# Attention scores of two softmax maps computed as couples, with 64-row matmuls for the small terms

## The chip, the cores and the metric

The kernel runs on one core of a Trainium2 chip. Its engines work side by side and are held together by semaphores: TensorE (PE) multiplies matrices into PSUM, VectorE (DVE), ScalarE (ACT) and GpSimd (POOL) work on rows, SyncE (SP) issues most of the DMAs. The metric is the device time of one execution in microseconds (us).

## What is computed

One encoder layer is applied to two sequences, of 2048 and of 1024 tokens, with the same weights. Its parts are an input projection, a convolution branch, an attention branch, a gated merge, an output projection and a layer norm. The change concerns the attention branch, which has 4 heads; each has two maps of scores over 64 features, and values of 128 features:

```python
def block(q_blk):
    s = jnp.einsum('bqhcd,bkhcd->bhcqk', q_blk, k).astype(jnp.float32) * scale
    p = jax.nn.softmax(s, axis=-1)
    a = p[:, :, 0] - lam * p[:, :, 1]
    return jnp.einsum('bhqk,bkhe->bqhe', a.astype(v.dtype), v)
```

## The kernel before

The kernel has three stages. The first projects the inputs and leaves queries, keys, values and gates in device memory. The second is the attention, from about 1437 to 2150 us of the profiled execution. The third merges and projects. Only the second is touched, and the loads that it makes.

**Numbers in two halves.** TensorE multiplies in a format with fewer bits than float32. So each operand is split into a high half (rounded to that format) and a low half (what is left). Queries and keys are stored as such halves in `qd` and `kd`, by half, then 128 rows (64 of map 0, 64 of map 1), then tokens.

**Scores.** `Head.keys` loads for a map `c` and 1024 keys a tile `km`: the high half on the upper 64 partitions, the low half on the lower 64. `Pair.load` loads for each map two tiles `qq` of 256 queries: the high half twice, one copy above the other, and the low half twice. `score(p, j, c, hf)` (lines 798 to 812) takes 128 queries (`j` = 0 or 1 of a pair), one map `c` and 1024 keys (`hf`). It makes four matmuls into the PSUM tile `s` (1024 columns, two buffers): for each 512 columns one with the high queries and one with the low ones, each over all 128 rows. So all four products of halves are summed, low times low among them. VectorE then scales `s`, takes the running maximum and writes it into the tile `e` (line 810), an eviction.

**Softmax and difference.** `soften` (line 821) takes the exponential on ScalarE with the sum of the row. `combine` (lines 824 to 830) takes the reciprocal of the sum of map 1 on VectorE (line 827); GpSimd multiplies it with the sum of map 0 (828), scales the tile of map 1 (829) and adds it to the tile of map 0 (830). From then on only the tile of map 0 is needed.

**Product with the values.** `turn` (line 832) transposes 256 keys of both query tiles of a pair on TensorE into `tp` (PSUM, two buffers), and ScalarE copies the high half into `ah` (839). `rest` (844) makes the low half `al` on VectorE. `product` makes six matmuls with the values into `ops` through `mm3` (lines 99 to 101). `squares` and `sums` take the sums of squares that the later norm needs.

**Buffers of scores.** `e` has `NE` = 8 buffers of 2048 columns. In the long group (2048 keys, 32 pairs of query tiles, 8 steps each) each map of each query tile has a buffer of its own. That of map 1 comes free when line 830 has read it; that of map 0, when the last turn of its pair has. A tile that is written into a used buffer waits on its engine until the former use is over. In the short group (16 pairs, 4 steps each) both maps lie in one buffer. `live[0]` counts the buffers that are taken, in the order in which the work is written.

**The order.** The `while` loop writes the order of TensorE, VectorE, ScalarE and GpSimd by hand (`manual_schedule`); each engine works strictly in it. A pass, or step, `now`, issues in this order: a score if one is left and `live` allows it; the turn of an earlier pair with its `ah`; what waits in `mid` for this step (exponentials); the product of the turn two steps earlier; the `al` of this step's turn; and what waits in `late` (a `combine`, `sums`). `p.at` says when a pair's turns may begin: `LAGS` steps after its last score. The exponential comes one step after its last score, `combine` at the end of the step after that. Every fourth step a piece of the next stage's weights is loaded and split (`resident`), for the first 128 steps.

Of the kernel before, what the change touches and what calls it, by code (L numbers as in the profile page):

```python
# [11 lines left out]
F32 = mybir.dt.float32  # L12
F32R = mybir.dt.float32r
AF = mybir.ActivationFunctionType
ALU = mybir.AluOpType
# [3 lines left out]
P = 128  # L19
# [7 lines left out]
HD = 64  # L27
# [4 lines left out]
EPS = 1e-5  # L32
SCALE = 1.0 / math.sqrt(HD)
KAPPA = 2.0 ** -11
LAGS = (8, 8)
NE = 8
NST = NH * sum(LENS) // P
ROOT_MAX = 1.8446742e19
# [5 lines left out]
def encoder_kernel(ctx: ExitStack, tc: tile.TileContext, t: dict):  # L44
    nc = tc.nc
# [25 lines left out]
    qd, kd, vd, sd, sr, ud, cgd, agd, mcd, mad, ogd, ssqd, rrd = ([] for _ in range(13))  # L71
# [34 lines left out]
    kvp, vp = [], []  # L106

    class Head:
# [4 lines left out]
        def keys(self, c):  # L113
            for hf in range(LENS[self.g] // 1024):
                self.km[c, hf] = kk = kvp[0].tile([P, 1024], F32R, name="km", bufs=6)
                for i in range(2):
                    nc.sync.dma_start(kk.bitcast(F32)[i * HD:(i + 1) * HD],
                                      kd[self.g][self.h][i, c * HD:(c + 1) * HD, hf * 1024:(hf + 1) * 1024])

        def values(self):  # L120
# [6 lines left out]
    class Pair:  # L127

        def __init__(self, g, h, qp):
            self.g, self.h, self.qp, self.L = g, h, qp, LENS[g]  # L130
            self.steps, self.lag = self.L // 256, LAGS[g]
            self.at, self.e, self.mx, self.qt = 10 ** 6, {}, {}, []
            self.col = col0[g][h] + 2 * qp

        def load(self, head, maps=(0, 1), queue=nc.sync):
            self.km, self.vv = head.km, head.vv
            for c in maps:
                for i in range(2):
                    qq = kvp[0].tile([P, 256], F32R, name=f"qq{c}{i}", bufs=2)
                    for r in range(2):  # L140
                        queue.dma_start(qq.bitcast(F32)[r * HD:(r + 1) * HD, :],
                                          qd[self.g][self.h][i, c * HD:(c + 1) * HD, self.qp * 256:self.qp * 256 + 256])
                    self.qt.append(qq)

    pairs = [Pair(g, h, qp) for g in range(2) for h in range(NH) for qp in range(LENS[g] // 256)]

# [3 lines left out]
    with ExitStack() as st:  # L150
# [10 lines left out]
        ws, ns, cu = (right.enter_context(tc.tile_pool(name=n, bufs=b, side="right", reuse_waits="tile"))  # L161
                      for n, b in (("a_s", 6), ("a_n", 5), ("a_u", 2)))
# [7 lines left out]
        def later(n, f):  # L170
            at[tick[0] + n].append(f)
# [278 lines left out]
        def combine(b):  # L450
            jobs.extend((13, combine_x, (b, k)) for k in range(4))
            start()
# [335 lines left out]
    with ExitStack() as st:  # L788
        pool = lambda **k: st.enter_context(tc.tile_pool(reuse_waits="tile", **k))
        sm = pool(name="b_sm", bufs=4)  # L790
        ap_ = pool(name="b_at", bufs=3)
        vp.append(pool(name="b_v", bufs=6))
        ep = pool(name="b_e", bufs=NE)
        psS = pool(name="b_s", bufs=2, space=PSUM)
        psT = pool(name="b_t", bufs=2, space=PSUM)
        psO = pool(name="b_o", bufs=2, space=PSUM)

        def score(p, j, c, hf):
            if hf == 0:
                if c == 0 or p.L == 2048:  # L800
                    p.tile = ep.tile([P, 2048], F32, name="e")
                p.e[j, c] = p.tile[:, c * p.L % 2048:][:, :p.L]
                p.mx[j, c] = sm.tile([P, 2], F32, name="mx")
            mx = p.mx[j, c]
            s = psS.tile([P, 1024], F32, name="s")
            for n in range(2):
                for i in range(2):
                    nc.tensor.matmul(s[:, n * 512:(n + 1) * 512], p.qt[2 * c + i][:, j * P:(j + 1) * P],  # L808
                                     p.km[c, hf][:, n * 512:(n + 1) * 512], start=i == 0, stop=i == 1)
            nc.vector.tensor_scalar(p.e[j, c][:, hf * 1024:(hf + 1) * 1024], s, -SCALE,  # L810
                                    mx[:, hf - 1:hf] if hf else None, op0=ALU.mult, op1=ALU.min,
                                    accum_out=mx[:, hf:hf + 1])

        def soften(p, j, c):
            nh = p.L // 1024
            e = p.e[j, c]
            if c == 0:
                sc = stats[:, p.col + j:p.col + j + 1]
            else:
                sc = sm.tile([P, 1], F32, name="ssum")  # L820
            nc.scalar.activation(e, e, AF.Exp, bias=p.mx[j, c][:, nh - 1:nh], scale=-1.0, accum_out=sc)  # L821
            return sc
# [62 lines left out]

        todo, ready = [], []
        for p in pairs:
            todo += [(p, j, c, hf) for j in range(2) for c in range(2) for hf in range(p.L // 1024)]
            ready += [(p, i) for i in range(p.steps)]
        eng = mybir.EngineType  # L890
        with tc.manual_schedule(engines={eng.PE, eng.DVE, eng.Activation, eng.Pool}):
            pieces = resident()
            cin = None
            now, before, live = 0, [], [0]
            kv[0, 0].values()
            early, mid, late, held = defaultdict(list), defaultdict(list), defaultdict(list), None
            while todo or ready or before or mid or late:
                now += 1
                for f in early.pop(now, ()):
                    f()  # L900
                if todo and (todo[0][3] or live[0] < NE):
                    p, j, c, hf = todo.pop(0)
                    live[0] += hf == 0 and (c == 0 or p.L == 2048)
                    if (j, c, hf) == (0, 0, 0):
                        nxt = pairs.index(p) + 1
                        if nxt < len(pairs):
                            x = pairs[nxt]
                            if (x.g, x.h) not in kv:
                                kv[x.g, x.h] = Head(x.g, x.h)
                                for i in range(2):  # L910
                                    kv[x.g, x.h].keys(i)
                                kv[x.g, x.h].values()
                            x.load(kv[x.g, x.h])
                    score(p, j, c, hf)
                    if (j, c, hf) == (1, 1, p.L // 1024 - 1):
                        p.at = now + p.lag
                    if hf == p.L // 1024 - 1:
                        def f(p=p, j=j, c=c, now=now):
                            sc = soften(p, j, c)
                            if c == 1:  # L920
                                def f():
                                    combine(p, j, sc)
                                    live[0] -= p.L == 2048
                                late[now + 2].append(f)
                        mid[now + 1].append(f)
                for again in range(2):
                    cur = None
                    if ready and ready[0][0].at + ready[0][1] <= now:
                        w, kg = ready.pop(0)
                        cur = w, kg, *turn(w, kg)  # L930
                        live[0] -= kg == w.steps - 1 and 2
                    if not again:
                        for f in mid.pop(now, ()):
                            f()
                    if before and (len(before) > 1 or not cur):
                        w, kg = before[0][:2]
                        product(*before.pop(0))
                        if kg == w.steps - 1:
                            sq = squares(w)
                            gap = 2 if w.g == 0 and not w is pairs[NH * LENS[0] // 256 - 1] else 1  # L940
                            for i in range(1, 4):
                                mid[now + i * gap].append(lambda sq=sq: next(sq))
                            if held:
                                late[now + 1 + gap].append(lambda p=held, w=w: sums(p, w))
                            held = w
                            if w is pairs[-1]:
                                late[now + 4].append(lambda w=w: sums(w, w))
                    if cur:
                        before.append((*cur[:2], cur[3], rest(*cur[2:])))
                    if not (ready and ready[0][0].at + ready[0][1] < now):  # L950
                        break
                if now % 4 == 0:
                    next(pieces, None)
                if not todo and cin is None:
                    kv_stack.close()
                    cin = cin_stack.enter_context(tc.tile_pool(name="c_in", bufs=2, side="right", reuse_waits="tile"))
                    ahead = prepare(rows[0], "u")
                    for i in range(CT + 2):
                        late[now + 2 * i].append(lambda: next(ahead))
                for f in late.pop(now, ()):  # L960
                    f()
# [177 lines left out]
```

## Time and profile before

| | us |
|---|---|
| median of three executions | 2713.28 |
| lowest, highest | 2706.08, 2713.36 |
| profiled execution, whole | 2720.08 |
| its span, first to last instruction | 2718.3 |
| scores on TensorE, line 808 (1280 matmuls of 512 columns) | 355.1 busy |
| evictions on VectorE, line 810 (192 first halves, 128 second) | 233.5 + 164.1 busy |
| exponentials, line 821 | 329.3 busy |
| `combine` on GpSimd, lines 829 and 830 | 170.7 + 372.7 busy |

In the views that follow, a line of the timeline has the start and the duration in us, the engine, the line of the kernel, the operation, what it writes and reads, and, in brackets, the idle time of the engine before it with what ended it. Matmuls overlap each other, so that the distance of their starts is what one costs. A line of the windows view has for one stretch the busy time and the number of instructions of TensorE, its weight loads, VectorE, ScalarE and GpSimd, then the granted clock of TensorE (1.00 is full speed), the busy share of the DMA engines and the GB/s. A line of the waits has the engine and line that waited, what it waited for, the total, how often, and the longest.

### The profile page before, as it was taken

How to read it: one execution, taken by the hardware profiler on the slowest of the kernel's cores; microseconds unless marked ns; L12 is line 12 of the kernel's file. 1: busy time of each engine (PE TensorE's matmuls, PEld its weight loads, DVE VectorE, ACT ScalarE, POOL GpSimd, SP SyncE). 2: the span in 40 equal slices, each digit the busy share in tenths (PEclk: the TensorE clock that was granted, in tenths of full speed). 3: DMA queues.
4: the chain of work that ended last, by engine and by line, in shares of the span. 5: the costliest groups of instructions: out<-in, count | busy, mean ns of one | idle time of the engine just before them, and what ended most of it. 6: DMA issues, size and time to landing. Idle time of an engine off the chain costs nothing.

```text
span 2718.3 us, 37893 instructions
## 1 busy us (share of the span) xinstructions
PE 2596.5 (96%) x12546; PEld 2111.8 (78%) x12546; DVE 2094.5 (77%) x2766; ACT 1196.3 (44%) x1957; POOL 1437.7 (53%) x957
## 2 busy tenths in 40 slices
PE   6999899999999999999987999999999999999998
PEld 3877688787778877778765888888888778777877
DVE  6699888779888349997546888888878776658665
ACT  4323333432232333442434888877789622222221
POOL 3577644235422113433545999888889633343343
PEclk6999999999999999999988999999999999999999
DMA  5578876868996775776866141413153575556553
GB/s 183 198 255 302 282 233 224 298 211 300 300 310 211 253 254 187 248 250 204 301 188 189 59 117 55 108 40 102 40 132 88 152 247 188 190 185 227 170 169 109
DMA packets 339572, 527.15 MB, mean 194 GB/s; under 512 B 42176, under 2 KB 126640, under 8 KB 339376
## 3 DMA queue, kind: packets, MB, share of 16 engines
q1 hardware_dynamic: 338736, 524.20, 59.5%
q8 instruction: 100, 1.64, 0.3%
q14 instruction: 96, 0.79, 0.1%
q10 hardware_dynamic: 640, 0.52, 0.1%
HBM read 344.00 MB, written 167.99 MB: 188 GB/s over the span
## 4 chain that ended last, share of the span: by engine, by line
PE 59%; DVE 10%; DMA 10%; issue 4%; ACT 2%; POOL 2%; SPq 2%; DVEq 0%; ACTq 0%; POOLq 0%
PE s L808 10%; PE pv L575 6%; PE pz L575 6%; PE px L575 5%; PE tp L837 5%; DVE acc L335 3%; PE y L99 3%; PE y L100 3%; PE y L101 3%; PE ops L99 3%; PE ops L101 3%; PE ops L100 3%; PE py L575 3%; PE z L99 2%; PE z L100 2%
## 5 line engine op out<-in xcount | busy, mean ns | idle before, releaser
L229 POOL TENSOR_TENSOR wl<-wq,wh 128x512 fp32r<-128x512 f32 x198 | 268.2, 1358 | 601.5 <-ACT wh L228 530.9
L335 DVE SCALAR_TENSOR_TENSOR acc<-uc,conv_dw,acc 128x1024 f32<-128x1024 f32 (+1 forms) x348 | 444.4, 1277 | 4.1
L830 POOL TENSOR_TENSOR e<-e 128x2048 f32<-128x2048 f32 (+1 forms) x96 | 372.7, 3882 | 8.0
L808 PE MATMUL s<-km,qq 128*128 128x512 f32 x1280 | 355.1, 400 | 17.3 <-DVE e L810 7.0
L821 ACT ACTIVATE e<-e,mx 128x2048 f32<-128x2048 f32 (+1 forms) x192 | 329.3, 1715 | 6.4 <-DVE e L810 6.3
L844 DVE TENSOR_TENSOR al<-tp,ah 128x512 fp32r<-128x512 f32 x320 | 220.2, 689 | 61.6 <-ACT ah L839 61.2
L808 PEld LDWEIGHTS s<-km,qq 128*128 128x128 f32 x1280 | 222.3, 191 | 53.6 <-DVE e L810 15.6
L810 DVE TENSOR_SCALAR_CACHE_REDUCE e<-s 128x1024 f32<-128x1024 f32 x192 | 233.5, 1216 | 26.4 <-PE s L808 25.5
L575 PE MATMUL pv<-xh,wh 128*128 128x512 f32 x528 | 219.0, 415 | 34.3 <-DVE ta L589 24.6
L839 ACT ACTIVATE ah<-tp 128x512 fp32r<-128x512 f32 x320 | 188.8, 592 | 93.6 <-PE tp L837 91.6
L575 PE MATMUL px<-xh,wh 128*128 128x512 f32 x528 | 212.0, 402 | 9.2 <-ACT xh L275 5.4
L575 PE MATMUL pv<-xh,wl 128*128 128x512 f32 x528 | 216.0, 409 | 0.7 <-POOL wl L229 0.3
L575 PE MATMUL pv<-xl,wh 128*128 128x512 f32 x528 | 215.9, 409 | 0.3 <-DVE xl L276 0.3
L575 PE MATMUL px<-xh,wl 128*128 128x512 f32 x528 | 211.4, 400 | 4.9 <-POOL wl L229 4.9
L575 PE MATMUL pz<-xh,wh 128*128 128x512 f32 x528 | 212.1, 402 | 2.4 <-ACT xh L275 1.5
L575 PE MATMUL pz<-xh,wl 128*128 128x512 f32 x528 | 211.1, 400 | 1.1 <-DMA wl<-wsd_0l 0.8
L575 PE MATMUL px<-xl,wh 128*128 128x512 f32 x528 | 210.8, 399 | 0.0
L575 PE MATMUL pz<-xl,wh 128*128 128x512 f32 x528 | 210.0, 398 | 0.7 <-DVE xl L276 0.7
L94 POOL TENSOR_TENSOR zl<-zraw,zh 128x512 fp32r<-128x512 f32 x88 | 124.3, 1415 | 159.0 <-ACT zh L93 145.9
L99 PE MATMUL ops<-ah,vv 128*128 128x256 f32 x640 | 207.7, 325 | 0.2 <-ACT row L870 0.2
L837 PE MATMUL tp<-ident,e 128*128 128x128 f32 x1280 | 193.4, 274 | 4.7 <-DVE al L844 3.7
L837 PEld LDWEIGHTS tp<-ident,e 128*128 128x128 f32 x1280 | 158.6, 141 | 49.3 <-DVE al L844 7.0
(221 smaller groups left out, 6336.0 us busy)
## 6 DMA issues: line engine op xcount, KB each, us to landing
wq<-in_w_in SPq DMA_DIRECT2D x220, 256.0 KB
qq<-qd SPq DMA_DIRECT2D x376, 64.0 KB
zraw<-in_w_out SPq DMA_DIRECT2D x88, 256.0 KB
ev<-ev SPq DMA_DIRECT2D x192, 64.0 KB
kd<-ev SPq DMA_DIRECT2D x48, 256.0 KB
qd<-ev SPq DMA_DIRECT2D x48, 256.0 KB
vd<-ev SPq DMA_DIRECT2D x48, 256.0 KB
mcd<-ev SPq DMA_DIRECT2D x48, 256.0 KB
```

Of the source, the lines that this page charges most:

```text
L99: nc.tensor.matmul(ps, ah, bh, start=first, stop=False)
L100: nc.tensor.matmul(ps, al, bh, start=False, stop=False)
L229: (lo_engine or (nc.vector if i in summed and si else nc.gpsimd)).tensor_sub(lo, src, hi.bitcast(F32))
L335: nc.vector.scalar_tensor_tensor(dst, src, dw_sb[:, c, k:k + 1], acc, op0=ALU.mult, op1=ALU.add)
L575: nc.tensor.matmul(ps, w[a][:, k], X[o, k][x], start=fresh and k == a == x == 0, stop=k == 3 and x == 1, skip_group_check=not fresh)
L808: nc.tensor.matmul(s[:, n * 512:(n + 1) * 512], p.qt[2 * c + i][:, j * P:(j + 1) * P], p.km[c, hf][:, n * 512:(n + 1) * 512], start=i == 0 ...
L810: nc.vector.tensor_scalar(p.e[j, c][:, hf * 1024:(hf + 1) * 1024], s, -SCALE, mx[:, hf - 1:hf] if hf else None, op0=ALU.mult, op1=ALU.min, ...
L821: nc.scalar.activation(e, e, AF.Exp, bias=p.mx[j, c][:, nh - 1:nh], scale=-1.0, accum_out=sc)
L830: nc.gpsimd.tensor_add(e0, e0, e)
L837: nc.tensor.transpose(tp[:, i, j * P:(j + 1) * P], p.e[j, 0][:, kt * P:(kt + 1) * P], ident)
L839: nc.scalar.activation(ah, tp, AF.Copy)
L844: nc.vector.tensor_sub(al, tp, ah.bitcast(F32))
```

## The change

Scores of both maps are made together. In place of two steps with one map each there is a couple of steps: the odd one makes the scores of both maps for 1024 keys, the even one makes none; both make their turn and their product as before.

A couple has four matmuls over 128 rows (high queries times high and low keys, as before) and four over 64 rows (low queries times high keys). The product of two low halves is left out. For this the keys of map 1 lie the other way round, the high half below, and the low queries of both maps lie in one tile `ql`, map 0 above map 1: the two 64-row matmuls of an `n` work on different rows of the array and write different tiles. Both evictions follow the eight matmuls.

A score is begun only at odd steps and only if all its buffers are free by count: two for the long group, one for the short. The exponential of map 0 comes one step after the couple's last score, that of map 1 two steps after, `combine` at the end of the fourth step after. `LAGS` is 9 in place of 8.

```diff
-LAGS = (8, 8)
+LAGS = (9, 9)
...
                 for i in range(2):
-                    nc.sync.dma_start(kk.bitcast(F32)[i * HD:(i + 1) * HD],
+                    o = (i ^ c) * HD
+                    nc.sync.dma_start(kk.bitcast(F32)[o:o + HD],
                                       kd[self.g][self.h][i, c * HD:(c + 1) * HD, hf * 1024:(hf + 1) * 1024])
...
             for c in maps:
-                for i in range(2):
-                    qq = kvp[0].tile([P, 256], F32R, name=f"qq{c}{i}", bufs=2)
-                    for r in range(2):
-                        queue.dma_start(qq.bitcast(F32)[r * HD:(r + 1) * HD, :],
-                                          qd[self.g][self.h][i, c * HD:(c + 1) * HD, self.qp * 256:self.qp * 256 + 256])
-                    self.qt.append(qq)
+                qq = kvp[0].tile([P, 256], F32R, name=f"qq{c}", bufs=2)
+                for r in range(2):
+                    queue.dma_start(qq.bitcast(F32)[r * HD:(r + 1) * HD, :], qd[self.g][self.h][0, c * HD:(c + 1) * HD, q])
+                self.qt.append(qq)
+            if maps[-1]:
+                self.ql = kvp[0].tile([P, 256], F32R, name="ql", bufs=2)
+                queue.dma_start(self.ql.bitcast(F32), qd[self.g][self.h][1, :, q])
...
-        def score(p, j, c, hf):
...
+        def score(p, j, hf):
+            q, ns, ss = slice(j * P, (j + 1) * P), [slice(n * 512, (n + 1) * 512) for n in range(2)], []
+            for c in range(2):
+                if hf == 0:
+                    if c == 0 or p.L == 2048:
+                        p.tile = ep.tile([P, 2048], F32, name="e")
+                    p.e[j, c] = p.tile[:, c * p.L % 2048:][:, :p.L]
+                    p.mx[j, c] = sm.tile([P, 2], F32, name="mx")
+                ss.append(psS.tile([P, 1024], F32, name="s"))
+                for n in ns:
+                    nc.tensor.matmul(ss[c][:, n], p.qt[c][:, q], p.km[c, hf][:, n], start=True, stop=False)
+            for n in ns:
+                for c in range(2):
+                    r = slice(c * HD, (c + 1) * HD)
+                    nc.tensor.matmul(ss[c][:, n], p.ql[r, q], p.km[c, hf][r, n], start=False, stop=True)
+            for c in range(2):
+                mx = p.mx[j, c]
+                nc.vector.tensor_scalar(p.e[j, c][:, hf * 1024:(hf + 1) * 1024], ss[c], -SCALE,
+                                        mx[:, hf - 1:hf] if hf else None, op0=ALU.mult, op1=ALU.min,
+                                        accum_out=mx[:, hf:hf + 1])
...
-            todo += [(p, j, c, hf) for j in range(2) for c in range(2) for hf in range(p.L // 1024)]
+            todo += [(p, j, hf) for j in range(2) for hf in range(p.L // 1024)]
...
-                if todo and (todo[0][3] or live[0] < NE):
-                    p, j, c, hf = todo.pop(0)
-                    live[0] += hf == 0 and (c == 0 or p.L == 2048)
+                if todo and now % 2 and (todo[0][2] or live[0] + todo[0][0].L // 1024 <= NE):
+                    p, j, hf = todo.pop(0)
+                    live[0] += 0 if hf else p.L // 1024
...
+                        def f(p=p, j=j, now=now):
+                            soften(p, j, 0)
+
+                            def f():
+                                sc = soften(p, j, 1)
+
                                 def f():
                                     combine(p, j, sc)
                                     live[0] -= p.L == 2048
-                                late[now + 2].append(f)
+                                late[now + 4].append(f)
+                            mid[now + 2].append(f)
                         mid[now + 1].append(f)
```

More of the change, by code (lines that the diff above doesn't have):

```diff
@@ L136, in load @@
             self.km, self.vv = head.km, head.vv
+            q = slice(self.qp * 256, self.qp * 256 + 256)
             for c in maps:
-                for i in range(2):
-                    qq = kvp[0].tile([P, 256], F32R, name=f"qq{c}{i}", bufs=2)
-                    for r in range(2):
-                        queue.dma_start(qq.bitcast(F32)[r * HD:(r + 1) * HD, :],
-                                          qd[self.g][self.h][i, c * HD:(c + 1) * HD, self.qp * 256:self.qp * 256 + 256])
-                    self.qt.append(qq)
+                qq = kvp[0].tile([P, 256], F32R, name=f"qq{c}", bufs=2)
[5 more added lines that the diff above has]
+                queue.dma_start(self.ql.bitcast(F32), qd[self.g][self.h][1, :, q])
     pairs = [Pair(g, h, qp) for g in range(2) for h in range(NH) for qp in range(LENS[g] // 256)]
@@ L796, in encoder_kernel @@
         psO = pool(name="b_o", bufs=2, space=PSUM)
-        def score(p, j, c, hf):
[L799 to L812, printed above, removed]
+        def score(p, j, hf):
[18 more added lines that the diff above has]
+                                        accum_out=mx[:, hf:hf + 1])
         def soften(p, j, c):
@@ L900, in encoder_kernel @@
                     f()
-                if todo and (todo[0][3] or live[0] < NE):
-                    p, j, c, hf = todo.pop(0)
-                    live[0] += hf == 0 and (c == 0 or p.L == 2048)
-                    if (j, c, hf) == (0, 0, 0):
+                if todo and now % 2 and (todo[0][2] or live[0] + todo[0][0].L // 1024 <= NE):
+                    p, j, hf = todo.pop(0)
+                    live[0] += 0 if hf else p.L // 1024
+                    if (j, hf) == (0, 0):
                         nxt = pairs.index(p) + 1
@@ L913, in encoder_kernel @@
                             x.load(kv[x.g, x.h])
-                    score(p, j, c, hf)
-                    if (j, c, hf) == (1, 1, p.L // 1024 - 1):
-                        p.at = now + p.lag
+                    score(p, j, hf)
                     if hf == p.L // 1024 - 1:
-                        def f(p=p, j=j, c=c, now=now):
-                            sc = soften(p, j, c)
-                            if c == 1:
+                        if j:
+                            p.at = now + p.lag
+                        def f(p=p, j=j, now=now):
+                            soften(p, j, 0)
+                            def f():
+                                sc = soften(p, j, 1)
                                 def f():
```

## The prediction

> **What bounds the kernel now.** I read the page first, then the busy time of each engine in three stretches of the attention stage, then the order of its instructions.
>
> ```profile
> span 2718.3 us, 37893 instructions
> ```
> ```profile
> core 0: us, PE busy (x) PEld busy (x) DVE busy (x) ACT busy (x) POOL busy (x), PEclk, DMA share, GB/s
> 1500.00:1550.00 50.00, 50.00 (x339) 44.48 (x338) 45.57 (x81) 42.18 (x66) 47.59 (x28) 1.00 0.19 56
> 1800.00:1850.00 50.00, 50.00 (x339) 44.45 (x338) 44.33 (x79) 39.74 (x60) 42.65 (x22) 1.00 0.22 60
> 2050.00:2100.00 50.00, 50.00 (x343) 44.46 (x342) 43.74 (x81) 46.65 (x95) 47.41 (x41) 1.00 0.34 96
> ```
>
> The change touches only this stage (about 1437 to 2150 us). TensorE never idles in these stretches, but GpSimd is at 95%, 85% and 95%, VectorE at 87 to 91%: whatever TensorE gives up, little can be collected. A step (one pass of the `while` loop) reads so on TensorE (start, duration):
>
> ```profile
> 1605.33 1.07 PE L808 MATMUL s<-km,qq 128*128 128x512 f32 x4
> 1606.24 0.60 PE L837 MATMUL tp<-ident,e 128*128 128x128 f32 x4
> 1606.60 0.37 PE L99 MATMUL ops<-ah,vv 128*128 128x256 f32 x1
> ...
> 1607.40 1.09 PE L808 MATMUL s<-km,qq 128*128 128x512 f32 x4
> 1608.33 0.60 PE L837 MATMUL tp<-ident,e 128*128 128x128 f32 x4
> ```
>
> Starts count, since ends overlap: scores 0.93 us (1607.40 to 1608.33, so 0.2325 a matmul), turn and product together 1.14 to 1.16 (1606.24 to 1607.40), a step 2.07. A pair of query tiles of the long group takes 8 steps; I number them 1 to 8. The second `combine` of a pair begins with these two reciprocals, 12 pairs apart:
>
> ```profile
> 1600.42 0.16 DVE L827 RECIPROCAL cc<-ssum 128x1 f32<-128x1 f32 x1
> ...
> 1802.74 0.15 DVE L827 RECIPROCAL cc<-ssum 128x1 f32<-128x1 f32 x1
> ```
>
> 202.32/12 = **16.86 us a pair**, which is 8 x 2.07 and the two small matmuls of `sums`.
>
> **The change, part by part.** *Scores.* A couple of steps had 8 matmuls of 128 rows; it gets 4 of them and 4 of 64 rows. No row shows a 64-row matmul. Bounds: two of them beside each other cost one slot (couple 6 x 0.2325 = 1.40 us, 0.46 less) or each its own (1.86, nothing less). I take 1.40, because two are on different rows and write different tiles, and keep 1.86. Changes of matmul kind cost between nothing (turn after scores, above) and 0.09 us (first product matmul 0.37 against 0.28 us); I take nothing.
>
> The Trainium skill ("TensorEngine Tiling (Array Packing)", Key Properties) says that different tiles run in parallel, but that a change of tiling mode drains TensorE. No run here shows either. By the first the serial rival below would fall away; by the second each couple pays two drains, and if one is like the 0.09 of the row above, the two couples on the chain below pay 0.36, some 10 us in all.
>
> *Loads.* Queries come by 5 DMAs a pair instead of 8, keys by as many as before:
>
> ```profile
> qq<-qd SPq DMA_DIRECT2D x376, 64.0 KB
> ```
>
> Nothing in the steady stage waits for them, so I count no gain. At the start the first couple needs both maps' keys, so two evictions that now run ahead wait behind a key load; a longer wait follows anyhow:
>
> ```profile
> 1442.73 1.19 PE L808 MATMUL s<-km,qq 128*128 128x512 f32 x4 [3.80 <-DMA km<-kd]
> ...
> 1457.54 4.56 PE L808 MATMUL s<-km,qq 128*128 128x512 f32 x12 [5.88 <-DMA qq<-qd]
> ```
>
> Without that cover it costs two evictions, 2.4 us. I take 0.
>
> *Order.* This decides. Counted from the loop, both versions take 341 steps, a pair's turns begin at the same step (one fewer to its last scores, one more in `LAGS`), and each has the score tiles `e` in eight buffers. Before, a pair takes one at steps 1, 3, 5, 7; after, two at steps 1 and 5. Held at step 5, before it takes its own: four map-0 tiles of the two earlier pairs (their turns aren't done) and two of this pair: six. **The two free ones are the map-1 tiles that the previous pair's two `combine`s give back**, and the second of these is now issued at the end of step 3 (`late[now + 4]`). Before, it is issued at the end of step 2, step 5 takes the other tile, and its own is first used at step 7, five steps or 10.4 us later. After, both are needed at step 5. What VectorE and GpSimd take:
>
> ```profile
> 1811.11 0.69 DVE L844 TENSOR_TENSOR al<-tp,ah 128x512 fp32r<-128x512 f32 x1 [0.58 <-ACT ah L839]
> 1811.72 0.15 DVE L827 RECIPROCAL cc<-ssum 128x1 f32<-128x1 f32 x1
> 1811.79 1.21 DVE L810 TENSOR_SCALAR_CACHE_REDUCE e<-s 128x1024 f32<-128x1024 f32 x1
> 1812.92 0.09 DVE L810 DVE_READ_ACCUMULATOR e<-s 128x1 f32 x1
> 1812.92 0.69 DVE L844 TENSOR_TENSOR al<-tp,ah 128x512 fp32r<-128x512 f32 x1
> 1813.52 1.28 DVE L810 TENSOR_SCALAR_CACHE_REDUCE e<-s,mx 128x1024 f32<-128x1024 f32 x1
> 1814.72 0.09 DVE L810 DVE_READ_ACCUMULATOR e<-s,mx 128x1 f32 x1
> ```
> ```profile
> 1812.02 0.19 POOL L828 TENSOR_TENSOR cc<-cc,stats 128x1 f32<-128x1 f32 x1 [1.93 <-DVE cc L827]
> 1812.31 2.08 POOL L829 TENSOR_SCALAR e<-e,cc,neglam 128x2048 f32<-128x2048 f32 x1
> 1814.47 4.62 POOL L830 TENSOR_TENSOR e<-e 128x2048 f32<-128x2048 f32 x1
> ```
>
> From start to start, VectorE needs 0.60 for an `al`, 0.07 for the reciprocal, 1.13 for an eviction of a first half and 1.20 for one of a second. From the reciprocal (1811.72) to the end of line 830 (1819.09) are 7.37 us. Between the reciprocal of step 3 and the second eviction of step 5 VectorE has 0.07 + 0.60 + 1.13 = 1.80 us of work. So **that eviction waits 5.6 us**, once a pair, and all that VectorE has behind it waits too: the `al`s of steps 5 and 6, the evictions of step 7, and through them TensorE's scores of step 7, since both `s` buffers are then full.
>
> Call the reciprocal R = 0; the wait ends at 7.45 (0.08 for the signal, my estimate between 0.03 from a turn's end at 1608.93 to its copy, below, and 0.15 from the reciprocal's end at 1811.87 to GpSimd's start). Behind it VectorE alone needs, to the next R: 1.13, two `al` 1.20, step 7's evictions 2.40, `al` 0.60, reciprocal 0.07, `al` 0.60, step 1's evictions 2.26, two `al` 1.20, step 3's 2.40 and `al` 0.60, together 12.46. **No pair is then shorter than 19.9 us.** Other engines stretch it:
>
> ```profile
> 1812.56 2.00 ACT L821 ACTIVATE e<-e,mx 128x2048 f32<-128x2048 f32 x1
> 1814.46 0.19 ACT L821 ACTIVATION_READ_ACCUMULATOR e<-e,mx 128x1 f32 x1
> 1814.55 0.59 ACT L839 ACTIVATE ah<-tp 128x512 fp32r<-128x512 f32 x1
> 1815.94 0.60 ACT L839 ACTIVATE ah<-tp 128x512 fp32r<-128x512 f32 x1 [0.80 <-PE tp L837]
> 1816.43 2.00 ACT L821 ACTIVATE e<-e,mx 128x2048 f32<-128x2048 f32 x1
> ```
> ```profile
> 1608.96 0.60 ACT L839 ACTIVATE ah<-tp 128x512 fp32r<-128x512 f32 x1 [0.68 <-PE tp L837]
> ```
> ```profile
> 1803.70 0.38 ACT L856 ACTIVATE ot<-ops 128x256 f32<-128x256 f32 x1
> 1803.97 2.01 ACT L821 ACTIVATE e<-e,mx 128x2048 f32<-128x2048 f32 x1
> ```
>
> On ScalarE an exponential takes 1.99, `ah` 0.49 before another operation and 0.62 until its `al` starts, `ot` 0.27; `ah` follows the start of its turn by 0.63. Step 7's second map can be scored from 8.73 (eviction 7.45 + 1.22 and the signal); four matmul slots 0.93 and turn and product 1.14 put step 8's turn at 10.80, its `ah` at 11.44. Then, in ScalarE's written order: `ah` 0.49, exponential 1.99, `ah` (waits for TensorE until 14.0) 0.49, exponential 1.99, `ot` 0.27, `ah` 0.62; so the `al` of step 2 starts at 17.4, and after it 0.60 + 2.40 + 0.60 lead to the next R at **21.0**.
>
> TensorE meanwhile idles from about 3.3 (first map of step 7 scored) to 8.7. What such a gap does to the granted clock:
>
> ```profile
> 2038.00:2042.00 4.00, 0.59 (x6) 0.39 (x4) 3.76 (x11) 2.17 (x5) 1.03 (x2) 0.88 0.31 93
> 2042.00:2046.00 4.00, 4.00 (x15) 3.51 (x16) 3.36 (x6) 3.99 (x8) 3.81 (x5) 0.50 0.19 52
> ```
> ```profile
> 2041.91 2.08 PE L808 MATMUL s<-km,qq 128*128 128x512 f32 x4 [3.41 <-DVE e L810]
> ```
>
> After 3.41 us idle four score matmuls took 2.08 instead of 1.09 us, at a clock of 0.50. After the 5.88 us gap at 1457.54 twelve took 4.56 where 11 x 0.2325 + 0.40 = 2.96 are due: 1.6 us lost. A 5.4 us gap lies nearest to that, and the 2.3 us of TensorE work between it and the end of step 8's turn are on the chain. I add 1.6: **22.6 us a pair**. The bounds are 21.0 (no loss) and 24.8 (half clock over all the 2.3 us and the couple behind, 1.2 more, and 64-row matmuls one after another, 1.0 more).
>
> *Sum.* The wait meets pairs 2 to 31, counted from 0 (before that buffers are unused): 30 waits, 29 periods. 29 x (22.6 - 16.86) = 166.5, and 5.6 for the first: **172 us more**. The short group keeps both maps in one buffer that only turns give back, which TensorE's order settles; there GpSimd (47.41 of 50) binds, and I take 0. The profiled execution was 2720.08 us outside, 2718.3 inside, the median of three 2713.28. On the median: **2885 us**; profiled, about 2892.
>
> **The rivals.** *The 64-row matmuls don't run beside each other* (the change doesn't do what it says). The eviction wait stays; step 8's turn stands behind one such couple and step 1's `ah` behind a second, 0.46 us each at full clock, so a pair takes about 1.0 longer: 29 x 1.0 = 29 more, 2914. Nothing in the trace speaks against it. *The buffers don't bind* (another is free). Then the nearest loop is turn to turn: step 8's turn, by the ScalarE chain above (3.17 + 0.49 + 1.99 + 0.27 + 0.62 to the `al`), VectorE 0.60 + 2.40 + 0.60, reciprocal to line 830's end 7.37, signal 0.08: 17.6 a pair, 0.73 x 30 = 22 more, 2735. Against it speaks the count. *Faster*: if neither chain binds, TensorE's 4 x 0.46 a pair are collected down to the next engine. GpSimd's 47.59 of 50 leaves 16.0 a pair while weights are split (16 pairs), later TensorE's 15.0: 16 x 0.8 + 14 x 1.8 = 38 less, 2675. It decides from the point where the second `combine` ends before VectorE asks for its buffer, that is with a reciprocal 5.6 us earlier. For it speaks today's trace:
>
> ```profile
> DVE e L810 <- PE s L808: 29.0, 77, 6.6
> ```
>
> Evictions now wait for scores, for no buffer. But the one spare buffer that gives them this is what taking two at once uses up.
>
> **How the numbers follow.** Forecast 0.72, serial 64-row matmuls 0.13, turn loop 0.08, faster 0.05, something between these two, within 0.3%, 0.02. About 0.3% (8 us) is what a measurement of this kernel can tell from no change. The range goes from the floor of 19.9 a pair, 29 x 3.04 + 5.6 = 94, so 2807, to 24.8 a pair, 29 x 7.94 + 5.6 = 236, 2949, and 10 more for 0.09 us at each change of matmul kind: 2807 to 2959. It leaves out the turn loop and the faster case. Faster 0.05, within 0.3% 0.03, slower 0.92.
>
> **What would show it.** Right: among the waits, VectorE's eviction held by GpSimd's line-830 operation some 30 times for about 5.6 us each; reciprocals 22 to 23 us apart; granted clock under 1.00 across the long group; GpSimd's busy time unchanged. A pair of 64-row matmuls starting almost together shows the parallel rows. Wrong: no such wait, or `e` evictions still waiting only for scores; then a wait of the turns for GpSimd would point to 2735, and a busy GpSimd without gaps to 2675. If the gaps exist but the clock stays at 1.00, the time is near 21.0 a pair, 2839.

## The result, and the profile after

| | before | after |
|---|---|---|
| median of four executions each, one chip (us) | 2709.78 | 2930.44 |
| lowest, highest | 2706.08, 2713.36 | 2928.25, 2932.15 |
| profiled execution, whole and span | 2720.08, 2718.3 | 2930.53, 2928.4 |

The change makes the kernel slower: 1.0816 times the time of before, with a 95% interval of 1.0797 to 1.0836. The forecast was 2885 us, in a range of 2807 to 2959. The direction and the place were right; the size was 45 us short.

In the page after, the eviction (line 820, 810 before) and the first scores (line 813) have these groups. The columns behind the bars are busy time with the mean of one in ns, and idle time before them with its releaser:

```profile
L820 DVE TENSOR_SCALAR_CACHE_REDUCE e<-s 128x1024 f32<-128x1024 f32 x192 | 229.9, 1223 | 214.0 <-POOL e L840 149.2
L813 PE MATMUL s<-km,qq 128*128 128x512 f32 x640 | 209.1, 440 | 160.2 <-DVE e L820 156.9
```

The view of the waits, over the whole run:

```profile
DVE e L820 <- POOL e L840: 149.2, 30, 5.0
PE s L813 <- DVE e L820: 156.9, 43, 4.8
```

VectorE's eviction waits for line 840 (830 before), the second operation of `combine`, 30 times; that is once in each of pairs 2 to 31, and 4.97 us on average. TensorE waits behind it. The windows of before showed 50.00 of 50 us of TensorE at a clock of 1.00; two of the same stretches after:

```profile
1500.00:1550.00 50.00, 40.60 (x246) 31.07 (x245) 31.59 (x55) 30.27 (x48) 34.59 (x20) 0.86 0.11 32
1800.00:1850.00 50.00, 40.56 (x237) 30.84 (x236) 30.58 (x54) 28.07 (x42) 30.16 (x16) 0.84 0.25 68
```

TensorE has some 240 matmuls in 50 us where it had 339, no other engine has more than 70% to do, and the clock is 0.84 to 0.86. That is what a loop of waits looks like: nothing is full. The timeline of one pair shows the loop. VectorE after:

```profile
1910.28 0.15 DVE L837 RECIPROCAL cc<-ssum 128x1 f32<-128x1 f32 x1
1910.35 0.67 DVE L854 TENSOR_TENSOR al<-tp,ah 128x512 fp32r<-128x512 f32 x1
1911.35 1.23 DVE L820 TENSOR_SCALAR_CACHE_REDUCE e<-s 128x1024 f32<-128x1024 f32 x1 [0.32 <-PE s L817]
1912.50 0.08 DVE L820 DVE_READ_ACCUMULATOR e<-s 128x1 f32 x1
1917.59 1.23 DVE L820 TENSOR_SCALAR_CACHE_REDUCE e<-s 128x1024 f32<-128x1024 f32 x1 [5.01 <-POOL e L840]
```

GpSimd in the same pair:

```profile
1910.88 2.06 POOL L839 TENSOR_SCALAR e<-e,cc,neglam 128x2048 f32<-128x2048 f32 x1
1913.02 4.53 POOL L840 TENSOR_TENSOR e<-e 128x2048 f32<-128x2048 f32 x1
```

Line 840 ends at 1917.55 and the eviction starts at 1917.59, 7.31 us behind the reciprocal. TensorE's first matmuls behind its own gap:

```profile
1918.88 1.22 PE L813 MATMUL s<-km,qq 128*128 128x512 f32 x2 [4.74 <-DVE e L820]
```

The same pair in windows cut at the gap:

```profile
1910.20:1918.80 8.60, 3.94 (x28) 2.85 (x26) 3.27 (x8) 4.77 (x8) 6.79 (x3) 0.93 0.06 16
1918.80:1924.30 5.50, 5.42 (x21) 4.12 (x22) 4.24 (x9) 0.90 (x2) 0.73 (x1) 0.50 0.17 52
1924.30:1934.10 9.80, 9.80 (x69) 7.85 (x68) 7.36 (x14) 8.05 (x11) 6.87 (x3) 0.99 0.04 13
```

After the gap TensorE works for 5.5 us at half clock, and then at full clock until the next gap. So a pair costs twice: the gap, and the work behind it.

Where the 210 us between the two spans lie: the reciprocal of the second `combine` comes once a pair, so 28 periods lie between two of them. After:

```profile
1504.63 0.15 DVE L837 RECIPROCAL cc<-ssum 128x1 f32<-128x1 f32 x1
...
2173.12 0.15 DVE L837 RECIPROCAL cc<-ssum 128x1 f32<-128x1 f32 x1
```

Before, the same two of the row:

```profile
1500.22 0.15 DVE L827 RECIPROCAL cc<-ssum 128x1 f32<-128x1 f32 x1
...
1971.75 0.15 DVE L827 RECIPROCAL cc<-ssum 128x1 f32<-128x1 f32 x1
```

A pair takes 668.49/28 = 23.875 us where it took 471.53/28 = 16.840. These 28 periods are 197.0 us of the difference. Ahead of them lie 4.4, the last pair of the long group adds 6.9, the short group 1.5, and all the rest 0.3.

### The profile page after: what moved, and what is told of

Read it like the earlier page. It is cut to its first block, busy times and chain, and to the rows that moved or that the text cites. A ratio compares the mean times of both kernels' runs of the same rounds, so it can differ in the third digit from the quotient of the medians.

```text
span 2928.4 us, 37721 instructions
## 1 busy us (share of the span) xinstructions
PE 2665.9 (91%) x12546; PEld 2088.0 (71%) x12546; DVE 2089.8 (71%) x2766; ACT 1201.1 (41%) x1957; POOL 1437.1 (49%) x957
## 5 line engine op out<-in xcount | busy, mean ns | idle before, releaser
L813 PE MATMUL s<-km,qq 128*128 128x512 f32 x640 | 209.1, 440 | 160.2 <-DVE e L820 156.9
L813 PEld LDWEIGHTS s<-km,qq 128*128 128x128 f32 x640 | 112.9, 206 | 201.0 <-DVE e L820 189.0
L847 PE MATMUL tp<-ident,e 128*128 128x128 f32 x1280 | 228.7, 308 | 3.7 <-DVE al L854 2.5
L99 PE MATMUL ops<-ah,vv 128*128 128x256 f32 x640 | 221.2, 346 | 0.0
```

The lines of the kernel that those rows point to most:

```text
L99: nc.tensor.matmul(ps, ah, bh, start=first, stop=False)
L813: nc.tensor.matmul(ss[c][:, n], p.qt[c][:, q], p.km[c, hf][:, n], start=True, stop=False)
L847: nc.tensor.transpose(tp[:, i, j * P:(j + 1) * P], p.e[j, 0][:, kt * P:(kt + 1) * P], ident)
```

## The experiments

The theory: the second eviction of step 5 needs the buffer that the previous pair's second `combine` gives back, too late by about 5 us; the gap on TensorE that follows halves the clock behind it. Rivals: a loop through the turns, GpSimd's throughput, and 64-row matmuls that don't run side by side. All edits are made to the changed kernel. Like it, they leave out the product of the two low halves, except the fifth and the tenth, which have it again. Each is compared with the kernel before, run beside it on the same chip.

| experiment | median (us) | ratio to before, 95% | us a pair |
|---|---|---|---|
| the change | 2930.44 | 1.0797 to 1.0836 | 23.88 |
| 1 nine buffers | 2747.13 | 1.0127 to 1.0169 | 17.68 |
| 2 combine one step earlier | 2791.85 | 1.0287 to 1.0334 | 19.52 |
| 3 both | 2721.63 | 1.0036 to 1.0075 | 17.18 |
| 4 gap filled | 2863.25 | 1.0555 to 1.0604 | 21.49 |
| 5 as 3, 128 rows | 2736.07 | 1.0064 to 1.0105 | 17.45 |
| 6 as 3, other order | 2723.48 | 1.0034 to 1.0071 | 17.18 |
| 7 exponentials apart | 2707.62 | 0.9980 to 1.0001 | 16.59 |
| 8 as 7, turns later | 2715.32 | 1.0010 to 1.0033 | 16.79 |
| 9 as 7, same rows | 2773.17 | 1.0201 to 1.0249 | 18.25 |
| 10 as 7, 128 rows | 2728.21 | 1.0036 to 1.0076 | 16.89 |

The time a pair is counted between reciprocals as above.

### 1. A ninth buffer

```diff
-NE = 8
+NE = 9
```

> The changed kernel with nine e buffers in place of eight, nothing else. Theory (VectorE's second eviction of a pair's step 5 waits for the buffer that GpSimd's combine still reads): the 30 waits of about 5.0 us for GpSimd vanish; what then holds a pair is the loop from turn to turn, 17.6 us by the prediction's rows and about 17.9 with the couple of scores at the 1.66 us that the changed kernel's trace shows; so about 2740 us, 1.01 of the kernel before. Rival (the couples or the 64-row matmuls are slow in themselves, or the clock is lower for another reason): still 2880 or more.

Measured: 2747.13 us. In the waits between 1500 and 2160 us the eviction no longer waits for GpSimd at all; the turns do:

```profile
PEld tp L847 <- POOL e L840: 33.4, 30, 1.2
PE tp L847 <- POOL e L840: 26.8, 30, 1.0
```

One more buffer takes back 183 of some 220 us, so the buffer is the cause. What is left is the next loop, that of the turns, which the prediction had as a rival: 17.6 us a pair worked out, 17.68 measured.

### 2. The combine one step earlier

```diff
-                                late[now + 4].append(f)
+                                late[now + 3].append(f)
```

> The changed kernel with combine at the end of the third step after a couple's last score instead of the fourth, eight buffers. Theory: its reciprocal stands two evictions and one al (3.0 us) earlier on VectorE, so 2.0 us of the 5.0 us wait are left; TensorE's gap falls to about 1.6 us, the clock stays at 1.00, and a pair takes 18.4 instead of 23.9 us: about 2757 us. Rival (the place of the combine doesn't matter, GpSimd's speed does): within 10 us of 2930.

Measured: 2791.85 us, 35 us more than expected. The wait itself came as expected, 2.0 us on average:

```profile
DVE e L820 <- POOL e L840: 57.7, 29, 2.1
```

But the pairs are of two lengths. Windows of one pair each:

```profile
1563.05:1583.05 20.00, 18.30 (x117) 14.49 (x115) 14.87 (x28) 14.34 (x22) 15.78 (x9) 0.91 0.13 41
1583.05:1601.49 18.44, 16.74 (x117) 12.88 (x115) 14.77 (x28) 14.35 (x22) 15.81 (x9) 1.00 0.62 151
```

The same instructions take 18.44 us at full clock, as long as was expected, or 20.00 us at 0.91. The timeline of TensorE behind the gap, in the long pair and in the short one:

```profile
1571.65 0.73 PE L813 MATMUL s<-km,qq 128*128 128x512 f32 x2 [1.70 <-DVE e L820]
...
1574.02 0.41 PE L100 MATMUL ops<-ah,vv 128*128 128x256 f32 x1
...
1591.65 0.73 PE L813 MATMUL s<-km,qq 128*128 128x512 f32 x2 [1.70 <-DVE e L820]
...
1593.59 0.28 PE L100 MATMUL ops<-ah,vv 128*128 128x256 f32 x1
```

Both gaps are 1.70 us, both bursts begin at full clock, and only in the first the product is at half clock 2.4 us later. The miss is the clock: I had counted on none being lost with so short a gap.

What decides between the two pairs is where the gap lies in time. In this trace every stretch of half clock between 1500 and 2080 us lasts 3.41 us, and these stretches begin multiples of 3.413 us apart (six of them from 1552.64 to 1573.12, eleven from 1668.69 to 1706.24). Windows cut on this grid, around the gap of the long pair and then around that of the short one:

```profile
1569.70:1573.12 3.42, 1.72 (x9) 0.74 (x8) 2.54 (x6) 1.48 (x3) 1.49 (x3) 1.00 0.25 77
1573.12:1576.53 3.41, 3.41 (x17) 3.41 (x17) 3.06 (x5) 1.26 (x3) 3.22 (x3) 0.50 0.25 77
...
1586.77:1590.18 3.41, 3.18 (x26) 2.55 (x22) 1.26 (x3) 3.29 (x7) 3.41 (x1) 1.00 0.51 151
1590.18:1593.60 3.42, 1.95 (x12) 1.22 (x13) 3.02 (x6) 1.00 (x3) 1.38 (x4) 1.00 1.04 215
1593.60:1597.01 3.41, 3.41 (x25) 2.58 (x23) 3.18 (x6) 3.09 (x4) 3.33 (x2) 1.00 0.83 209
```

In the long pair the whole gap lies in one stretch of the grid (1.72 us busy, 1.70 idle), and the next stretch is at half clock. In the short pair the grid cuts it into 0.23 and 1.47 us, and the clock stays. In that part of the trace half clock followed 20 stretches, with 1.57 to 1.80 us idle; it followed none with 1.53 or less, nor one with 1.69. The ends of matmuls are modelled, so that the border is rough.

The Trainium skill ("TensorE: Matmul & The Clock Gate", Why this matters for your kernels) advises against gaps of more than about 3 us between bursts, because one idle window brings the clock to half. The gap of 4.74 us after the change agrees; the gap of 1.70 us here, which halves the clock in some pairs, lies below that figure, and the measurement decides.

### 3. Both together

> Both edits: nine buffers and combine one step earlier. Theory: neither the buffer nor the turn loop (about 14.9 us) binds; TensorE does, with 4 couples of 1.66, 8 turns with products of 1.15 and 0.24 for the sums, 16.1 us a pair, against 16.86 before: about 2690 us, 0.99 of the kernel before. Rival (GpSimd's 16.0 us a pair while weights are split, with gaps, binds): about 2705 to 2715, no gain.

Measured: 2721.63 us. No eviction and no turn waits for GpSimd any more, yet it is 0.55% slower than before. Neither the expected 2690 nor the rival by GpSimd's load explains it, for GpSimd (the last busy time before the clock) isn't full in the two stretches used above, and the clock is 1.00:

```profile
1500.00:1550.00 50.00, 48.60 (x336) 37.63 (x333) 43.14 (x76) 41.26 (x63) 45.29 (x26) 1.00 0.16 48
1800.00:1850.00 50.00, 48.66 (x335) 37.66 (x335) 42.78 (x76) 39.66 (x61) 41.81 (x22) 1.00 0.12 36
```

The waits between 1500 and 2160 us show many short ones instead:

```profile
DVE al L854 <- ACT ah L849: 68.3, 82, 1.2
...
PEld s L813 <- DVE e L820: 35.7, 60, 2.5
...
PE s L813 <- DVE e L820: 13.3, 30, 0.5
```

Two evictions and two exponentials now come in one bunch, and VectorE, ScalarE and TensorE wait for each other around it. That was the next theory, tried in experiment 7.

### 4. The gap filled

Twenty more matmuls of map 0, overwritten by the real ones, stand ahead of them where the gap lies:

```diff
+                for n in ns * (10 if j == 1 and hf == 1 and c == 0 else 0):
+                    nc.tensor.matmul(ss[c][:, n], p.qt[c][:, q], p.km[c, hf][:, n], start=True, stop=True)
                 for n in ns:
                     nc.tensor.matmul(ss[c][:, n], p.qt[c][:, q], p.km[c, hf][:, n], start=True, stop=False)
```

> The changed kernel with 20 repeats of the first map's two 128-row matmuls before the real ones, in the second query tile's second half of the keys only: 4.65 us of TensorE work in the gap that the wait leaves; the scores are the same. Theory that the gap also costs clock: the wait stays at 5.0 us, the granted clock goes to nearly 1.00, a pair falls from 23.9 to about 21.3 us, so about 2855 us. Rival (the clock loss lies off the chain): no change, 2930, or more by what the repeats add.

Measured: 2863.25 us; with 20 more matmuls a pair it is 67 us faster than the change without them. The wait is still there (between 1500 and 2160 us; lines are two later), and the clock is 1.00 in the two stretches used above:

```profile
DVE e L822 <- POOL e L842: 146.9, 29, 5.1
```

So a pair's 23.88 us are 21.49 of chain at full clock and 2.39 of lost clock. The timeline of TensorE shows the chain behind the wait at full clock:

```profile
1924.81 0.73 PE L815 MATMUL s<-km,qq 128*128 128x512 f32 x2 [0.25 <-DVE e L822]
1925.47 0.74 PE L819 MATMUL s<-km,ql 64*128 64x512 f32 x4
1926.14 0.66 PE L849 MATMUL tp<-ident,e 128*128 128x128 f32 x4
```

From the scores of map 1 to the turn are 1.33 us, where the prediction had four slots, 0.93. The two matmuls over 128 rows take 0.66 to the next start, where two slots are 0.465.

### 5 and 6. The 64-row matmuls

The fifth is experiment 3 with the low queries copied twice again, as before the change, and the second four matmuls over 128 rows (the loads, and the index of `qt` in the first four, are left out here):

```diff
...
-                    r = slice(c * HD, (c + 1) * HD)
-                    nc.tensor.matmul(ss[c][:, n], p.ql[r, q], p.km[c, hf][r, n], start=False, stop=True)
+                    nc.tensor.matmul(ss[c][:, n], p.qt[2 * c + 1][:, q], p.km[c, hf][:, n], start=False, stop=True)
```

> The kernel of e3 (nine buffers, earlier combine) with the second four matmuls of a couple over all 128 rows again, as before the change, low times low included; couples and order stay. A couple then costs 8 x 0.2325 = 1.86 us on TensorE instead of the 1.66 that the traces of the changed kernel show (1.00 for four of 128 rows, 0.66 for four of 64). Theory (the 64-row matmuls run two beside each other, and the changes of kind take 0.27 of the 0.46 us back): 0.2 us a couple more, 0.8 us a pair, about 2745 us with the short group. Rival (the changes of kind eat the whole gain, or TensorE isn't what binds e3): 2722, no change.

Measured: 2736.07 us, a pair 0.27 us longer than in experiment 3, where 0.8 were expected: TensorE binds there only in part. The sixth is experiment 3 with another order, so that neighbours in the order lie on the same rows:

```diff
-            for n in ns:
-                for c in range(2):
+            for c in range(2):
+                for n in ns:
```

> The kernel of e3 with the four 64-row matmuls in another order: both of map 0, then both of map 1, so that neighbours on the queue often share their rows. Theory (only neighbours on different rows run beside each other): one pair of four still overlaps in part, the four cost 0.66 to 0.93 us, a pair of query tiles up to 1.1 us more: 2725 to 2760 us. Rival (the array runs any two that it can, whatever the order): 2722.

Measured: 2723.48 us, as experiment 3. In the trace of the change two of the four start at once, and then the other two; these are rows of short stretches, the first with the last matmul over 128 rows:

```profile
1901.83 0.39 PE L813 MATMUL s<-km,qq 128*128 128x512 f32 x1
1902.15 0.50 PE L817 MATMUL s<-km,ql 64*128 64x512 f32 x2
...
1902.48 0.40 PE L817 MATMUL s<-km,ql 64*128 64x512 f32 x2
```

With the order turned it is the same:

```profile
1807.00 0.50 PE L817 MATMUL s<-km,ql 64*128 64x512 f32 x2
```

So the written order doesn't decide, and it isn't the order in which they start. The trace marks the matmuls that signal VectorE, which are the last ones of the two maps; in all 160 couples of experiment 6 both marks stand on the two that start second. So the first of map 1 starts ahead of the second of map 0, which is written before it; what moves it is not shown. Whether different rows are what lets two start at once needed experiment 9.

### 7 and 8. The exponentials apart

The bunch of experiment 3 is drawn apart: the exponential of map 1 comes two steps after that of map 0, `combine` where the change has it, and as the tiles live longer there are ten buffers and the turns begin a step later.

```diff
-LAGS = (9, 9)
-NE = 8
+LAGS = (10, 10)
+NE = 10
...
-                            mid[now + 2].append(f)
+                            mid[now + 3].append(f)
```

> The changed kernel with ten buffers, LAGS of 10, and the exponential of map 1 three steps after the couple's last score instead of two (combine stays at four). e3's trace has VectorE wait 68 us for copies that ScalarE makes behind two exponentials in neighbouring steps. Theory: with the exponentials a step apart and turns one step later no loop is longer than TensorE's 16.1 us a pair, and GpSimd's 16.0 while weights are split: 16.1 to 16.5, about 2695 us, 0.995 of the kernel before. Rival (the two s buffers, freed together by two evictions in a row, hold TensorE whatever ScalarE does): 17.2 a pair as in e3, about 2720.

Measured: 2707.62 us over 12 executions, beside 2711.04 for the kernel before (23 executions); the interval of the ratio, 0.9980 to 1.0001, holds 1. In these two stretches TensorE no longer waits:

```profile
1500.00:1550.00 50.00, 50.00 (x352) 39.95 (x351) 45.41 (x81) 42.99 (x69) 48.13 (x28) 1.00 0.17 50
1800.00:1850.00 50.00, 50.00 (x351) 39.93 (x350) 44.75 (x79) 42.71 (x63) 44.19 (x22) 1.00 0.30 76
```

The 16.59 us a pair of the table are a mean. Of the 28 periods 25 take 16.16 to 16.45 us, as expected, and three take 17.71, 17.79 and 19.71. In these three ScalarE waits for a piece of the next stage's weights, and the copies `ah` that are written behind it come late, and with them `al` and the turn on TensorE:

```profile
1564.28 0.42 ACT L893 ACTIVATE w_conv_projh<-wraw 128x256 fp32r<-128x256 f32 x1 [3.17 <-DMA wraw<-in_w_conv_proj]
```

Over the last twelve periods, after the last of these weights, a pair takes 16.39 us where it took 16.90 before. So this is what the couples are worth once TensorE doesn't wait: 0.51 us a pair. Over 28 periods that would be 14 us; the trace has 7.0 of them and the medians differ by 3.4, which isn't clear of noise. Three edits were made at once, and which of them the bunch needed isn't shown.

The eighth has `LAGS = (11, 11)` on top, so that turns have more time.

> e7 with LAGS of 11. If the wait of the turns for GpSimd still cost something in e7, this takes it away, and the time falls below e7's; if not, it stays within 5 us of e7 (one more step at the end of each group adds 2 to 4 us).

Measured: 2715.32 us, 0.1 to 0.33% slower than before. Over the last twelve periods a pair takes 16.40 us, as in experiment 7; the longer mean comes from pairs in the part with the weights, of up to 19.85 us. More distance doesn't help.

### 9. All four on the same rows

Experiment 7, with the keys' high halves of both maps on the upper 64 partitions and the low queries of both maps beside each other there (two DMAs for them instead of one, left out here):

```diff
...
-                    o = (i ^ c) * HD
+                    o = i * HD
...
-                    r = slice(c * HD, (c + 1) * HD)
-                    nc.tensor.matmul(ss[c][:, n], p.ql[r, q], p.km[c, hf][r, n], start=False, stop=True)
+                    nc.tensor.matmul(ss[c][:, n], p.ql[:, c, q], p.km[c, hf][:HD, n], start=False, stop=True)
```

> The kernel of e7, where TensorE binds, with the high halves of both maps' keys on the upper 64 partitions and both maps' low queries there too, so that all four 64-row matmuls of a couple use the same rows of the array; the result is the same. In e6 the order of the four made no difference, which leaves open what lets two of them start together. Theory (different rows): none can overlap, the four cost 0.93 us and the change of kind on top, about 0.4 us a couple more than 0.66, 1.6 us a pair, about 2707 + 32 x 1.6 + 16 x 0.8 = 2770 us. Rival (a 64-row matmul takes half a slot wherever its rows are): 0.66 stays, 2707.

Measured: 2773.17 us, 3 from what was expected. TensorE's timeline:

```profile
1806.08 1.19 PE L817 MATMUL s<-km,ql 64*128 64x512 f32 x4
1807.20 0.66 PE L847 MATMUL tp<-ident,e 128*128 128x128 f32 x4
```

The four take 1.12 us to the next start. In the change, with the maps on different rows, they take 0.66:

```profile
1901.15 1.07 PE L813 MATMUL s<-km,qq 128*128 128x512 f32 x4
1902.15 0.73 PE L817 MATMUL s<-km,ql 64*128 64x512 f32 x4
1902.81 0.66 PE L847 MATMUL tp<-ident,e 128*128 128x128 f32 x4
...
1904.02 0.60 PE L847 MATMUL tp<-ident,e 128*128 128x128 f32 x4
...
1905.16 1.07 PE L813 MATMUL s<-km,qq 128*128 128x512 f32 x4
```

Different rows are what lets two run side by side; that is worth 0.46 us a couple and 65.6 us of the whole between experiments 7 and 9. Over the last twelve periods a pair takes 18.22 us, 1.83 more than in experiment 7, which is four times 0.46.

### 10. Experiment 7 with 128 rows

The edit of experiment 5, on experiment 7.

> The kernel of e7 with the second four matmuls of a couple over all 128 rows, low times low included. Theory: TensorE binds, a couple takes 1.86 instead of about 1.68, 0.7 us a pair: 16.6 becomes 16.9 to 17.3, about 2707 + 20 = 2727 us, so that the 64-row matmuls are worth some 20 us where nothing else holds TensorE. Rival (couples with another bound): 2707.

Measured: 2728.21 us, 20.6 more than experiment 7, and 0.30 us a pair (0.42 over the last twelve periods, with 16.81). That is what the 64-row matmuls, with the fewer loads that they need, are worth where TensorE binds. Couples without them are 0.36 to 0.76% slower than the kernel before; with them they are level with it. The 28 periods hold 1.4 us of what experiment 10 is slower than before; where the rest lies isn't traced.

## Why the prediction was right, and where its sizes were off

**The order decides** (right). The buffer, the eviction, the operation of GpSimd that it waits for, the 30 times and the pairs were named and found. Experiment 1 shows it as the cause: one more buffer, and the wait and the gaps of 4.7 us are gone.

**The wait**: 5.6 us predicted, 4.97 measured. Its end was right, 7.31 us behind the reciprocal instead of 7.45. VectorE was ready for it 2.30 us behind the reciprocal (1912.58) instead of 1.80, and 0.32 of that because the couple's scores, which the prediction had ready, came late (the bracket at 1911.35). That moved no time: the end of the wait sets the chain.

**The chain at full clock**: 21.0 predicted, 21.49 in experiment 4. The step that fell short is "Changes of matmul kind cost between nothing and 0.09 us; I take nothing". A couple's eight matmuls take 1.66 us (1901.15 to 1902.81 above) where 1.40 were predicted and 1.86 would be without a gain. About 0.1 us lies at each of three places, where a slot is 0.2325: ahead of the first two 64-row matmuls (0.32 from 1901.83 to 1902.15), between these and the other two (0.33 to 1902.48), and behind them (0.33 to 1902.81). The first and the third are the changes of kind, each at about the upper end of the prediction's range; the one between was in no term. The part on the chain behind the wait takes 1.33 instead of 0.93, with a fourth such tenth in the two 128-row matmuls right behind the wait (experiment 4). The turn behind the 64-row matmuls takes 1.21 with its product (1902.81 to 1904.02), the next 1.14.

The Trainium skill ("TensorEngine Tiling (Array Packing)", Key Properties) says that tiles run in parallel and that a change of tiling mode drains TensorE. The trace agrees with the first: two matmuls start at once. For the second it has the tenth of a microsecond at either change, but no run here separates a drain from another cost of a change, and the tenth between the two pairs of 64-row matmuls stands at no change.

**The clock** (right in kind, too small). The prediction added 1.6 us a pair, from the gap at 1457.54, and kept a larger loss as a bound. Measured are 23.88 - 21.49 = 2.39. The half clock lasts 6.83 us, two stretches of the grid of experiment 2, in both places. But after the gap at 1457.54 TensorE worked in 3.25 us of it (to 1460.79), and in the change in 5.55 (1918.88 to 1924.43); half of these are 1.6 and 2.8. So the whole way from the gap to step 8's turn ran at half clock. Step 8's `ah` follows the second reciprocal by 14.18 us (11.44 predicted without loss, 13.04 with 1.6), and by 11.85 in experiment 4. A pair of 23.88 us is also seven stretches of that grid long (7 x 3.413 = 23.89), and half clock begins at the same place in each pair (1893.71, 1917.60, 1941.50); whether the grid sets the length is not shown.

**The sum.** A pair came out at 23.88 instead of 22.6. Of the 1.28 us, 0.41 are the chain at full clock up to that `ah` (11.85 instead of 11.44), which is the couple; 0.73 are the clock (14.18 - 11.85 = 2.33, instead of 1.6), and 0.14 the chain from it to the next reciprocal (9.70 instead of 9.56). Times 29 that is 37 of the 38 us by which the profiled 2930.53 passes the 2892 predicted for it. The other 7 to the 45 on the median are no part of the mechanism: the profiled execution of before stood 6.8 above its median, that of after stands at it.

**At nothing** were put the loads, the start and the short group. The span holds 4.4 us more up to the first reciprocal quoted above, where 5.6 were predicted for the first wait, and 1.5 more for the short group. Right within 2 us.

**The rivals.** *64-row matmuls one after another*: fell, by the trace and by experiment 9. *The turn loop*: not what binds in the change, but it binds as soon as the buffer doesn't (experiment 1). *Faster, 2675*: its condition was met in experiment 7, its time wasn't, which reached 2707.62. The prediction collected 0.46 us a couple; a couple of steps of TensorE takes 4.01 (1901.15 to 1905.16) instead of 4.14 (two of 2.07), so all but 0.13 of it went to the three places above and to the turn behind, and TensorE stayed the limit. Four times 0.13 is the 0.51 us a pair of experiment 7.

## What to carry to other kernels

Count buffers at the point where they are taken, not only how many there are: two that are taken at once use up the spare one that hid a slow release, and then the release sits on the path of every pass. Price a gap on TensorE with the slow clock behind it; here each 5 us wait cost 2.4 us more. And before matrices are halved in rows, price the changes between kinds of matmul and the start of each group: of 0.46 us saved a couple, 0.13 were left.

## What the runs showed of the hardware that was not expected

- A gap of 1.70 us on TensorE halved the clock in some pairs and not in others, with the same instructions at the same distances (experiment 2). The clock changed on a grid of 3.41 us, and half clock came when 1.57 us or more of the gap lay in one stretch of it, with one exception at 1.69. Twenty useless matmuls a pair kept it at 1.00 and paid for themselves (experiment 4).
- 64-row matmuls on different rows start in twos whatever order they are written in (experiment 6); on the same rows four cost 1.12 instead of 0.66 us (experiment 9).
- Four 128-row and four 64-row matmuls cost 0.26 us more than the six slots that they fill: about 0.1 at each change of kind and 0.1 between the two pairs of 64-row ones. The turn behind takes 0.07 more.
